# Second mixer of a two-layer trunk: output weights split in dead tiles during the attention, and another written order of squares and products in the last projection

## The chip, the cores and the metric

One core of one Trainium2 chip runs the whole program. The metric is device microseconds of one launch. The kernel before took 1179.97 us (median of three runs, 1178.41 to 1181.39).

## The reference

A decoder trunk of two layers on a sequence of 512 tokens, model width 1024, float32. Each layer is `x = x + rms_norm(mixer(rms_norm(x)))` and then `x = x + rms_norm(conv_ffn(rms_norm(x)))`. The change lies in the mixer of the second layer:

```python
def odd_mixer(h, w_in, w_out):
    cq, ck, cv, sq, sk, sv = split_cols(h @ w_in, ODD_SPLITS)
    o_dil = dilated_attention(groups(cq), groups(ck), groups(cv), slopes)   # 3 groups x 4 heads
    o_sb = stick_breaking_attention(heads_first(sq, 4), heads_first(sk, 4), heads_first(sv, 4))
    return concatenate([heads_last(o_dil), heads_last(o_sb)], axis=-1) @ w_out   # (512 x 512) @ (512 x 1024)
```

`dilated_attention` makes three softmax attentions per head over strided windows (group 0 with stride 1, groups 1 and 2 with strides 4 and 16) and merges them by weights made from their denominators: "the merged groups". The first 256 rows of `w_out` belong to the merged groups, the last 256 to stick-breaking.

## The kernel before

Every float32 product is made as three products of two-part numbers. A weight tile (128 x 1024) is loaded by SP into one of three buffers `wraw`; ACT casts it to the high part (`Weights.split`, L71), DVE subtracts to get the low part (L72); `mm3` (L253 to L255) issues three matmuls. The stream of weights `W` has five pairs of buffers `wh`/`wl` and splits five units ahead. A weight buffer is free again when its last matmul has run, a `wraw` buffer when DVE has subtracted.

Tokens are four tiles of 128, taken in `ORDER` 3, 2, 1, 0. `odd()` runs: projections and stick-breaking attention (pool `sb`: `sq`, `sk`, `sv`, the mask, the large tiles `z` and `sp`); then groups 1 and 2 (`score12`, `turn12`, `value12`, with table `tab12`), with the remaining projections as fillers between them; then sixteen small transfers `on<-ob` that put their results in token order; then group 0 (`score0`, `turn0`, `value0`, `merged`, one token tile each, in a pipeline of four stages by `skewed`), with the value projection `apv` as filler. `merged` transposes the merged output of a token tile and splits it into `og`.

Then follows the last projection. For each token tile, `row_product` makes twelve matmuls (`ao`, 128 x 512) for each of two halves of the output columns: six with the stick-breaking output `oS` and the two units of weights that come from `W`, six with `oG` and the two units that a second stream `W2` splits. `W2` is written behind the attention and has its own pool `owx`, whose memory overlaps that of `sb`. For each half, `part_of` then squares the product on ACT (L224, with a sum along the row) and multiplies it by a gain on DVE (L227). Then come the root (`rstd`, POOL, L177 to L180), the residual `X` (DVE, L1204), the mean square of the new `X` (ACT, L187), and the normalised tile `t` (`normed`, DVE, L1183). Eight PE transposes of `t` (L210), ACT casts (L170) and DVE subtractions (L171) put it into `xh`/`xl`, from which the second FFN starts with the products `u`.

Order: outside `manual_schedule` blocks a scheduler orders each engine's instructions when the program is built; inside (the last projection, for PE, DVE, ACT and POOL) the written order holds among the block's own instructions, and the scheduler mixes earlier ones in between. Each engine runs its instructions in that order.

Of the kernel before, what the change touches and what calls it, by code (L numbers as in the profile page):

```python
# [9 lines left out]
F32 = mybir.dt.float32  # L10
# [6 lines left out]
P = 128  # L17
S = 512
# [67 lines left out]
def trunk(tc, A, out):  # L86
# [3 lines left out]
    with ExitStack() as top:  # L90
# [125 lines left out]
        def part_of(t, ms, n, a, g, between=None):  # L216

            c = slice(n * S, n * S + S)
            o = t[:, c]
            if isinstance(a, tuple):  # L220
                DVE.tensor_tensor(o, *a, ALU.subtract)  # L221
                a = o
            junk = chp.tile([P, D], BF16, tag="junk", name="junk", bufs=1)
            ACT.activation(junk[:, :S], a, AF.Square, scale=D ** -0.5, accum_out=ms[:, n:n + 1])  # L224
            if between:
                between()
            DVE.tensor_tensor(o, a, g[:, c], ALU.mult)  # L227

        def begin(pool=None, tag="s"):
            return ((pool or chp).tile([P, D], F32, tag=tag, name="t"),  # L230
                    chp.tile([P, 2], F32, tag="ms", name="ms2", bufs=4))
# [630 lines left out]
        def odd(xnT, pending):  # L862
            xh, xl = xnT
            with ExitStack() as es:
# [13 lines left out]
                with ExitStack() as e1:  # L878
                    sb = e1.enter_context(tc.tile_pool(name="sb", bufs=1, reuse_waits="tile"))
                    sq = [sb.tile([P, S], F32, tag=f"sq{u}", name=f"sq{u}") for u in range(2)]  # L880
                    sk = [sb.tile([P, S], F32, tag=f"sk{u}", name=f"sk{u}") for u in range(2)]
                    sv = sb.tile([P, NT, 256], F32, tag="sv", name="sv")
                    smask = sb.tile([P, S], F32, tag="smask", name="smask")
                    tri = sb.tile([P, 2, P], F32R, tag="tri", name="tri")
                    trif = sb.tile([P, 2, P], F32, tag="z", name="trif", bufs=2)
                    nc.scalar.dma_start(smask[:], A["sb_mask"])
                    nc.scalar.dma_start(trif[:], A["sb_tri"])
                    DVE.tensor_copy(tri[:], trif[:])

                    def proj_T(dst, scale, permuted, on_act):  # L890
                        acc = bank("a", "apt")
                        wh, wl = W.next()
                        for k in range(KD):
                            mm3(acc[:], wh[:, k * P:(k + 1) * P], wl[:, k * P:(k + 1) * P],
                                xh[:, k], xl[:, k], k == 0, k == KD - 1)
                        src, d = acc[:], dst[:]
                        if permuted:
                            src = src.rearrange("p (t r) -> p r t", r=4)
                            d = d.rearrange("p (r t) -> p r t", r=4)
                        if on_act:  # L900
                            ACT.activation(d, src, AF.Copy, scale=scale)
                        else:
                            DVE.tensor_scalar(d, src, scale, None, ALU.mult)

                    def proj_V(dst):
                        ws = [W.next() for _ in range(2)]

                        def tile_V(i):
                            t = slice(i * P, (i + 1) * P)
                            a = bank("a", "apv")  # L910
                            for k in range(KD):
                                wh, wl = ws[k // 4]
                                c = slice((k % 4) * 256, (k % 4 + 1) * 256)
                                mm3(a[:, :256], xh[:, k, t], xl[:, k, t], wh[:, c], wl[:, c], k == 0, k == KD - 1)
                            if i % 2:
                                DVE.tensor_copy(dst[:, i], a[:, :256])
                            else:
                                ACT.copy(dst[:, i], a[:, :256])

                        return tile_V  # L920


                    ws = [W.next() for _ in range(4)]
                    for i in ORDER:
                        t = slice(i * P, (i + 1) * P)
                        a = bank("a", "av12")
                        for k in range(KD):
                            if k == KD // 2 and pending:
                                pending.pop(0)()
                            wh, wl = ws[k // 2]  # L930
                            c = slice((k % 2) * 512, (k % 2 + 1) * 512)
                            mm3(a[:], xh[:, k, t], xl[:, k, t], wh[:, c], wl[:, c], k == 0, k == KD - 1)
                        st = sb.tile([P, 512], F32, tag="sp", name="vst", bufs=2)
                        ACT.copy(st[:], a[:])
                        for r in range(4):
                            nc.scalar.dma_start(cv12[32 * i:32 * i + 32, r], st[r::4, :])


                    for u in range(2):
                        proj_T(sq[u], 0.125, False, True)  # L940
                        proj_T(sk[u], 1.0, False, False)
                    tile_V = proj_V(sv)
                    for i in ORDER:
                        tile_V(i)
                    off = (0, 512, 896, 1152, 1280)
                    spans = ((0, 0, 512), (1, 512, 896), (2, 896, 1280))

                    def sb_scores(u):

                        zs = [sb.tile([P, 1280], F32, tag="z", name="z", bufs=2) for _ in range(2)]  # L950
                        for n, (j0, o0, o1) in enumerate(spans):
                            zp = [bank(t, "zp") for t in ("ss", "nt", "ss")[n]]
                            for j in (j0,) if j0 < 2 else (2, 3):
                                for y in range(2):
                                    r = slice(y * 64, y * 64 + 64)
                                    PE.matmul(zp[y][:, off[j] - o0:off[j + 1] - o0], sk[u][r, j * P:(j + 1) * P],
                                              sq[u][r, j * P:], start=True, stop=True)
                            for y in range(2):
                                for j in (j0,) if j0 < 2 else (2, 3):
                                    DVE.tensor_tensor(zs[y][:, off[j]:off[j + 1]], zp[y][:, off[j] - o0:off[j + 1] - o0],  # L960
                                                      smask[:, :S - j * P], ALU.add)

                        sps = []
                        for z in zs:
                            sp = sb.tile([P, 1280], F32, tag="sp", name="sp", bufs=2)
                            DVE.tensor_scalar(sp[:], z[:], 40.0, None, ALU.min)
                            ACT.activation(sp[:], sp[:], AF.Exp)
                            sps.append(sp)
                        return list(zip(zs, sps))

                    def sb_softplus(z, sp):
                        ACT.activation(sp[:], sp[:], AF.Ln, bias=1.0)
                        DVE.tensor_tensor(sp[:], z[:], sp[:], ALU.max)

                    def sb_weights(z, sp):
                        sh = sb.tile([P, 1280], F32R, tag="sh", name="sh")
                        sl = sb.tile([P, 1280], F32R, tag="sl", name="sl")
                        split(sh[:], sl[:], sp[:])

                        for j0, o0, o1 in spans:  # L980
                            zp = bank("ssn"[j0], "cp")
                            for j in (j0,) if j0 < 2 else (2, 3):
                                n = S - j * P
                                c = off[j] - o0
                                for j2 in range(j, NT):
                                    for part in (sh, sl):
                                        PE.matmul(zp[:, c + (j2 - j) * P:c + n], tri[:, 0 if j2 == j else 1],
                                                  part[:, off[j2]:off[j2 + 1]], start=(j2 == j and part is sh),
                                                  stop=(j2 == NT - 1 and part is sl))
                            DVE.tensor_tensor(z[:, o0:o1], z[:, o0:o1], zp[:, :o1 - o0], ALU.add)  # L990
                        ACT.activation(z[:], z[:], AF.Exp)
# [325 lines left out]
```

## Time and profile before

| | |
|---|---|
| median of 3 runs | 1179.97 us (1178.41 to 1181.39) |
| profiled execution, own time | 1178.65 us |
| its span, first to last instruction | 1176.9 us |
| PE busy | 1152.7 us (98%) |
| PE weight loads busy | 942.3 us (80%) |
| DVE busy | 811.3 us (69%) |
| ACT busy | 557.0 us (47%) |
| HBM read and written | 117.95 and 6.29 MB, 106 GB/s |

The profile times one execution; "idle before, releaser" says what ended an engine's idle time. Times such as 790.83 are microseconds from the start of the span. The last projection starts at 786.2 and the second FFN at 820.2. The 1.75 us between own time and span lie outside the instructions.

### The profile page before, as it was taken

The page shows a single profiled execution, that of the slowest core. Times are in us where ns is not written, and L with a number is a line of the kernel's source. Part 1 is how long each engine was busy: PE and PEld are TensorE (multiplying, and loading weights), DVE is VectorE, ACT ScalarE, POOL GpSimd, SP SyncE. Part 2 cuts the span into 40 slices and gives each one's busy share as a digit, 9 for nine tenths or more (in the row PEclk, how much of TensorE's full clock was granted, in tenths as well). Part 3 has the DMA queues.
Part 4 walks back from the last instruction along what each step waited for, and adds up shares of the span by engine and source line. Part 5 has one row for each costly group of instructions (what it writes and reads, how often), then busy time and mean ns, then how long its engine had stood idle before and what let it go on. Part 6 is the DMA issues. An engine that isn't in the chain of part 4 may idle for free. (4 is left out here: it accounts for less than half of the span.)

```text
span 1176.9 us, 15162 instructions
## 1 busy us (share of the span) xinstructions
PE 1152.7 (98%) x5656; PEld 942.3 (80%) x5656; DVE 811.3 (69%) x1424; ACT 557.0 (47%) x942; POOL 56.7 (5%) x139
## 2 busy tenths in 40 slices
PE   8999999999999999999999999999999999999997
PEld 7876766798888888888878877887988888888885
DVE  6677358657666766899873465476576766779896
ACT  5465246445444434456553454454444434345562
POOL 2100002310000000000020000002000000000001
PEclk9999999999999999999999999999999999999999
DMA  7320340033233332354735212222233232324461
GB/s 284 109 81 19 114 126 1 37 129 122 94 92 105 90 103 86 100 158 159 245 110 154 72 54 93 69 55 108 94 109 106 90 107 90 95 94 135 142 207 72
DMA packets 39049, 126.81 MB, mean 108 GB/s; under 512 B 4672, under 2 KB 6336, under 8 KB 38848
## 3 DMA queue, kind: packets, MB, share of 16 engines
q1 hardware_dynamic: 37056, 122.11, 32.5%
q10 hardware_dynamic: 1920, 3.74, 1.0%
q8 instruction: 44, 0.72, 0.3%
q14 instruction: 29, 0.24, 0.1%
HBM read 117.95 MB, written 6.29 MB: 106 GB/s over the span
## 5 line engine op out<-in xcount | busy, mean ns | idle before, releaser
L72 DVE TENSOR_TENSOR wl<-wraw,wh 128x1024 fp32r<-128x1024 f32 (+1 forms) x205 | 248.2, 1218 | 186.5 <-ACT wh L71 185.9
L71 ACT CAST wh<-wraw 128x1024 fp32r<-128x1024 f32 (+1 forms) x205 | 212.6, 1046 | 289.5 <-PE u L254 177.8
L253 PE MATMUL u<-xh,wh 128*128 128x512 f32 (+1 forms) x768 | 285.0, 372 | 1.0 <-ACT xh L170 1.0
L254 PE MATMUL u<-xl,wh 128*128 128x512 f32 (+1 forms) x768 | 285.2, 372 | 0.7 <-DVE xl L171 0.7
L255 PE MATMUL u<-xh,wl 128*128 128x512 f32 (+1 forms) x768 | 285.0, 371 | 0.0
L253 PEld LDWEIGHTS u<-xh,wh 128*128 128x128 f32 x768 | 144.5, 188 | 26.3 <-ACT xh L170 1.4
L254 PEld LDWEIGHTS u<-xl,wh 128*128 128x128 f32 x768 | 144.7, 188 | 25.7 <-DVE xl L171 0.9
L255 PEld LDWEIGHTS u<-xh,wl 128*128 128x128 f32 x768 | 144.7, 188 | 25.0
L255 PE MATMUL acc<-wh,gl 128*128 128x512 f32 x248 | 96.5, 389 | 0.0
L254 PE MATMUL acc<-wl,gh 128*128 128x512 f32 x248 | 96.5, 389 | 0.0
L253 PE MATMUL acc<-wh,gh 128*128 128x512 f32 x248 | 96.4, 390 | 0.0
L402 ACT ACTIVATE y<-u,cw 128x512 f32<-128x512 f32 x88 | 67.6, 775 | 1.7 <-PE u L255 1.7
L407 ACT ACTIVATE y<-y 128x512 f32<-128x512 f32 x44 | 27.7, 632 | 85.1 <-DVE y L405 85.1
L405 DVE SCALAR_TENSOR_TENSOR y<-u,cw,y 128x510 f32<-128x510 f32 x88 | 65.6, 747 | 2.5
L403 DVE SCALAR_TENSOR_TENSOR y<-u,cw,y 128x511 f32<-128x511 f32 x88 | 65.1, 743 | 0.9 <-ACT y L402 0.9
L253 PEld LDWEIGHTS acc<-wh,gh 128*128 128x128 f32 x248 | 46.6, 188 | 10.1 <-issue 0.5
L255 PEld LDWEIGHTS acc<-wh,gl 128*128 128x128 f32 x248 | 46.6, 188 | 9.8
L254 PEld LDWEIGHTS acc<-wl,gh 128*128 128x128 f32 x248 | 46.6, 188 | 9.6
L253 PE MATMUL apt<-xh,wh 128*128 128x512 f32 x128 | 50.6, 396 | 0.0
L254 PE MATMUL apt<-xl,wh 128*128 128x512 f32 x128 | 50.0, 391 | 0.0
L255 PE MATMUL apt<-xh,wl 128*128 128x512 f32 x128 | 49.9, 390 | 0.0
L177 POOL TENSOR_TENSOR rv<-ms,epst 128x1 f32<-128x1 f32 x40 | 11.5, 291 | 734.8 <-ACT junk L224 668.8
(287 smaller groups left out, 1910.8 us busy)
## 6 DMA issues: line engine op xcount, KB each, us to landing
wraw<-in_ffn_w_up SPq DMA_DIRECT2D x88, 512.0 KB, 3.6
wraw<-in_ffn_w_down SPq DMA_DIRECT2D x44, 512.0 KB, 3.6
wraw<-in_od_w_dqk SPq DMA_DIRECT2D x12, 512.0 KB, 3.7
wraw<-in_ffn_w_down SPq DMA_DIRECT2D x22, 256.0 KB, 2.6
wraw<-in_ev_w_dqk SPq DMA_DIRECT2D x8, 512.0 KB, 3.7
wraw<-in_ev_w_out SPq DMA_DIRECT2D x8, 512.0 KB, 3.8
spill<-X SPq DMA_DIRECT2D x8, 512.0 KB, 2.6
X<-spill SPq DMA_DIRECT2D x8, 512.0 KB, 6.2
```

The lines of the kernel that those rows point to most:

```text
L71: self.nc.scalar.copy(h[:, :w], raw[:, :w])
L72: self.nc.vector.tensor_tensor(l[:, :w], raw[:, :w], h[:, :w].bitcast(F32), ALU.subtract)
L177: POOL.tensor_tensor(v[:, :n], ms, epst[:, :n], ALU.add)
L253: PE.matmul(o, lh, rh, start=first, stop=False, skip_group_check=more)
L254: PE.matmul(o, lh, rl, start=False, stop=False, skip_group_check=more)
L255: PE.matmul(o, ll, rh, start=False, stop=last, skip_group_check=more)
L402: ACT.activation(y[:, z], u, AF.Identity, bias=c[:, 3:4], scale=c[:, 2:3])
L403: DVE.scalar_tensor_tensor(y[:, z, 1:], u[:, :S - 1], c[:, 1:2], y[:, z, 1:], ALU.mult, ALU.add)
L405: DVE.scalar_tensor_tensor(y[:, z, 2:], u[:, :S - 2], c[:, 0:1], y[:, z, 2:], ALU.mult, ALU.add)
L407: ACT.activation(y[:, 0], y[:, 0], AF.Silu)
```

## The change

Four edits, all around the last projection of the second mixer:

1. The pool `sb` lives until the end of the mixer (its `with` block goes, and the code loses one step of indentation). `sq` and `sk` become one tile each instead of two.
2. `W2` is called before group 0 is written, and its high and low parts go into tiles that are read no more by then: unit 0 into `sq` and `sk`, unit 1 into `sv` and `tab12`. The pools `owx` and `osc` go, with one `spacer`.
3. The rows' tiles `t` come alternately from `z` and `sp` of pool `sb` (two buffers each) instead of three buffers of `osc`.
4. In a row of the last projection, the first half's product with the gain (DVE) is written ahead of its square (ACT), and the mean square of the row before is written after the first half's square instead of at the end of its own row. For the last row it stands behind the loop.

```diff
-        def part_of(t, ms, n, a, g, between=None):
+        def part_of(t, ms, n, a, g, between=None, dve_first=False):
...
+            def product():
+                DVE.tensor_tensor(o, a, g[:, c], ALU.mult)
+
+            if dve_first:
+                product()
             junk = chp.tile([P, D], BF16, tag="junk", name="junk", bufs=1)
             ACT.activation(junk[:, :S], a, AF.Square, scale=D ** -0.5, accum_out=ms[:, n:n + 1])
             if between:
                 between()
-            DVE.tensor_tensor(o, a, g[:, c], ALU.mult)
+            if not dve_first:
+                product()
...
-                with ExitStack() as e1:
-                    sb = e1.enter_context(tc.tile_pool(name="sb", bufs=1, reuse_waits="tile"))
-                    sq = [sb.tile([P, S], F32, tag=f"sq{u}", name=f"sq{u}") for u in range(2)]
-                    sk = [sb.tile([P, S], F32, tag=f"sk{u}", name=f"sk{u}") for u in range(2)]
+                sb = es.enter_context(tc.tile_pool(name="sb", bufs=1, reuse_waits="tile"))
+                sq, sk = [[t[:, u] for u in range(2)] for t in (sb.tile([P, 2, S], F32, tag="sq", name="sq"),
+                                                                sb.tile([P, 2, S], F32, tag="sk", name="sk"))]
...
+                W2 = Weights(nc, None, [(A["od_w_out"][k], 1024) for k in range(2)], 2, wpool)
+                homes = [[(sb, "sq"), (sb, "sk")], [(sb, "sv"), (ap, "tab12")]]
+                W2.pair = lambda: [pool.tile([P, D], F32R, tag=tag, name="wo") for pool, tag in homes.pop(0)]
+                wo2 = [W2.next() for _ in range(2)]
                 tile_V = proj_V(cv)
                 skewed([[g(i) for g in (score0, turn0, value0, merged)] for i in ORDER],
                        [lambda i=i: tile_V(i) for i in ORDER])
...
-                wx = es.enter_context(tc.tile_pool(name="owx", bufs=2, reuse_waits="tile"))
-                W2 = Weights(nc, wx, [(A["od_w_out"][k], 1024) for k in range(2)], 2, wpool)
-                wout = [W2.next() for _ in range(2)] + [W.next() for _ in range(2)]
-                sc = es.enter_context(tc.tile_pool(name="osc", bufs=3, reuse_waits="tile"))
-                spacer(sc, 16)
                 g_post, g_next = gain("od_post_g", 0), gain("ffn_pre_g", 1)
+                wout = wo2 + [W.next() for _ in range(2)]
...
-                        t, ms = begin(sc, "t")
+                        t, ms = begin(sb, ("z", "sp")[n % 2])
                         row_product(acc, terms, True, True, (0,))
-                        part_of(t, ms, 0, acc[0], g_post)
+                        part_of(t, ms, 0, acc[0], g_post, dve_first=True)
                         if n > 1:
                             turns.pop(0)()
+                        if n:
+                            j, tj = norms.pop()
+                            rj = mean_square(X[j][:])
                         row_product(acc, terms, True, True, (1,))
                         part_of(t, ms, 1, acc[1], g_post)
                         r = rstd(ms[:, 0:1], ms[:, 1:2])
                         if n:
-                            normed(*norms.pop())
+                            normed(j, rj, tj)
                         DVE.scalar_tensor_tensor(X[i][:], t[:], r[:, 0:1], X[i][:], ALU.mult, ALU.add)
-                        norms.append((i, mean_square(X[i][:]), t))
+                        norms.append((i, t))
                         turns.append(turned(i, nx, "na", t))
+
+                    r = mean_square(X[i][:])
```

In the built order, the first unit's cast and subtraction stand between the first and the second round of groups 1 and 2, the second unit's cast ahead of the last of the four exponentials of the second round, and its subtraction ahead of the last two copies `ob<-o`. On SP the order becomes: all four loads of `od_w_out`, four loads of `ffn_w_up`, then the sixteen `on<-ob`. Before, it was: two loads of `od_w_out`, two of `ffn_w_up`, two of `od_w_out`, then `on<-ob`, then the other two of `ffn_w_up`. PE's matmuls are the same in number; the `ao` products of the first row stand a little otherwise among the last transposes.

## The prediction

> **What bounds the kernel now.** I read the page first: which engine has no idle time.
>
> ```profile
> PE   8999999999999999999999999999999999999997
> PEclk9999999999999999999999999999999999999999
> ```
>
> PE is busy nearly everywhere, so this change can gain only where PE waits or runs slowly, and DVE or ACT time matters only where PE waits for it. The chain that ended last covers only the kernel's last 10 us, so PE's waits and its timeline come next. In the answer on all waits of PE (line, who ended it, us in total, times, longest), five rows touch the end of the second mixer (the first one's longer wait, 0.8, is the first mixer's).
>
> ```profile
> PE ao L253 <- ACT wh L71: 1.3, 2, 0.8
> PE ao L254 <- DVE wl L72: 1.1, 1, 1.1
> PE u L253 <- ACT xh L170: 1.0, 1, 1.0
> PE u L254 <- DVE xl L171: 0.7, 1, 0.7
> PE tpo L1162 <- ACT pt L1124: 0.5, 1, 0.5
> ```
>
> PE's timeline there (start, length, instruction, idle before it):
>
> ```profile
> 789.88 0.44 PE L1123 MATMUL t<-ident,s 128*128 128x128 f32 x2
> 790.83 0.44 PE L1162 MATMUL tpo<-ident,m 128*128 128x128 f32 x2 [0.52 <-ACT pt L1124]
> 792.57 0.51 PE L253 MATMUL ao<-wh,og 128*128 128x512 f32 x1 [0.46 <-ACT wh L71]
> 794.22 0.79 PE L254 MATMUL ao<-wl,og 128*128 128x512 f32 x1 [1.15 <-DVE wl L72]
> ...
> 800.20 0.39 PE L253 MATMUL ao<-wh,osh 128*128 128x512 f32 x1
> ...
> 818.77 0.39 PE L255 MATMUL ao<-wh,og 128*128 128x512 f32 x1
> 820.16 0.74 PE L253 MATMUL u<-xh,wh 128*128 128x256 f32 x4 [1.01 <-ACT xh L170]
> 821.56 0.38 PE L254 MATMUL u<-xl,wh 128*128 128x256 f32 x1 [0.66 <-DVE xl L171]
> ```
>
> The first row of the projection waits twice for the weights that `W2` splits last; later the FFN waits for the last normalised tile. The stretches of 5 us (PE busy, loads, DVE, ACT, POOL, granted clock, DMA) show a third loss.
>
> ```profile
> 785.00:790.00 5.00, 4.93 (x38) 4.28 (x38) 3.54 (x17) 2.69 (x9) 0.00 (x0) 1.00 0.27 97
> 790.00:795.00 5.00, 2.88 (x15) 2.09 (x16) 4.39 (x8) 2.70 (x5) 0.10 (x1) 0.91 0.38 107
> 795.00:800.00 5.00, 5.00 (x21) 3.94 (x20) 2.26 (x6) 1.75 (x6) 0.19 (x1) 0.75 0.61 210
> ```
>
> After the waits the clock is halved from about 794.0 to 797.4: products start 0.43 us apart instead of 0.227, which costs 3.4 x 0.5 = 1.7 us, in "busy" time. All these losses are a few tenths of a per cent of the span.
>
> **Part 1, the early split.** Four 128x1024 operations move (casts 1.05 us, subtractions 1.22 us). Where they go:
>
> - Cast and subtraction of unit 0 stand ahead of a cast of `W` and the second round's scores. SP issues its load at 734.13, where one of `ffn_w_up` was issued before; with the page's 3.5 us to landing it is there at 737.7, cast at 738.8, subtracted at 740.0. The scores started at 740.78 and now start about 1.1 us later, their exponentials too. PE takes the result only at 747.37, the last exponential began at 743.42: nothing on the path.
> - The cast of unit 1 waits for a load that SP can issue only when unit 0's subtraction has freed `wraw` (740.0): landed 743.5, cast 744.6. Queued behind it on ACT is the fourth exponential (0.51), now done near 745.3, and behind that only PE's transposes at 747.37. Cover 2 us; each microsecond beyond costs one.
> - Its subtraction falls into DVE's idle 3.40 us after 761.98, ahead of the copies `ob<-o` at 765.39. It frees the `wraw` for a fourth load of `ffn_w_up`, issued near 763.2 and landed near 766.7, ahead of the sixteen `on<-ob`, whose issue at 766.22 waits for those copies anyway. Perhaps 0.5 us late; DVE's `mn` waits for them (0.68 us before). Queued behind `mn` are the next scores, whose exponentials ended 1.8 us before PE's transposes at 777.03. So nothing.
> - At 783.2 one cast of `W` now precedes the last tile's exponentials (0.25 us later) and one subtraction the copy of `pt` (1.2 us later, to 786.4). PE needs that copy at 787.5, after the three `ao` products and two transposes that the built order now has there: nothing.
>
> What is left for PE from 786.02 to the second row: 24 products x 0.2275 = 5.46; 24 `o` matmuls 1.70 + 0.85; six pairs of transposes 1.3; seven returns from these to 512-wide products at 0.08 (0.31 against 0.23 to the next start), 0.6. Sum 9.9, with no late input: `og` is ready at 788.7 by the rows of cast and subtraction, its product comes at 790.0, and the wait for `pt` (0.52) is covered by three products that now lie in between. Before, it took 800.20 - 786.02 = 14.2. **Gain 4.2**, of which 1.7 is the clock.
>
> A rule speaks against counting that last part: in the Trainium skill, "TensorE: Matmul & The Clock Gate", section on HAM oscillation, only idle gaps over about 3.4 us throttle. By it these gaps (longest 1.15) would have cost no clock, and part 1 would gain 2.5. The trace disagrees, and I take the trace.
>
> **Part 2, the written order.** Per row, from one `X` to the next, a chain runs through DVE and ACT: product 0.69, square 0.69, casts `xh` 0.94, mean square 1.23, square to second product 0.73, product 0.60, `normed` 1.32, `X` 1.20: 7.4 us with `xh`, 6.5 without, against PE's 24 x 0.2275 = 5.46 (6.3 with transposes). Before, `X` followed `X` at 6.4, 7.05 and 8.35 us (802.14, 808.54, 815.59, 823.94). I laid the built order out with these lengths, PE's last product of the first row at 795.8:
>
> - Row 2: no wait; row 1: the transposes at 804.2 find `t` ready with 0.1 to spare.
> - Row 0: the transposes are due at 810.6, `t` has its halves at 811.4 and 812.1: PE waits 1.2 us in all, 0.6 more than before. **Loss 0.6**; its last product starts at 815.2.
> - FFN: a weight buffer comes free only with the third product of the last half (813.5), ACT casts into it (1.0), then squares (0.69), then casts `xh` (815.75): PE idle 0.4, then 0.3 for `xl`; it runs freely at 816.5. Before, from last product to free run were 2.8 us (818.77 to 821.56), now 1.35. **Gain 1.4**.
> - In the FFN's first 10 us the last two tiles' transposes are due about when `t` is (one was moved 20 products later in the built order). Waits of 0.1 + 0.1 + 0.2, taken as **loss 0.4**; later than that nothing.
>
> Tiles `t` in other memory: `X` at L242 and L1204, from two pools, takes 1283 and 1278 ns; I take 0, between -0.1 and +0.1 us.
>
> **Sum:** -4.2 + 0.6 - 1.4 + 0.4 = -4.6. The profiled execution, 1178.65 us (span 1176.9 and 1.75 around it), becomes 1174.0. It lies 1.3 below the median of the runs; off that median it is 1175.4, my forecast. Bounds: every wait gone, -4.2 and the 1.95 of `u` and `tp` before, about -6.2; clock unsaved, chain losses doubled and nothing gained at the FFN's start, -4.6 + 1.7 + 1.0 + 1.4 = -0.5.
>
> **Rivals.**
> - *The chain on DVE and ACT replaces PE as bound in the last projection.* For: its 7.4 against PE's 6.3, and `t` is found ready with 0.1 to spare. Against: laid out, it waits only in row 0. If the last two rows slip 1.2 each, 2.4 of the gain go: 1177.8, within 0.3%.
> - *The clock halves in another place.* Before, the 3.4 us ahead of 794.1 had 1.6 idle and half clock followed; those up to 821.4 had 1.5 idle and it did not, so the margin is thin. PE now idles 1.9 us in all between 810.6 and 816.6, spread over 6 us. One such stretch costs 1.7: 1177.1. The same title of the Trainium skill, section "What's actually happening", has the gate look at free-running windows of 3413 ns, by which some runs of before might escape the half clock and be 1.7 faster; the fastest run is only 0.24 below the profiled one, so none here shows that.
> - *Slower: the second unit's cast blocks ACT.* Place: ACT's queue at 743.5. Behind the cast stand an exponential and all of PE's next transposes. The Trainium skill, "PSUM — Partial Sum Buffer", section on engine and sequencer instructions, has ACT's queue strictly in order; ACT's rows here never overtake either. It costs one for one from 745.6 on, and 1.7 more of clock. To end 3.6 above the median before, it must cost 4.6 + 3.6 = 8.2, 6.5 beside the clock: landed at 752.1, 12 us after issue. Against: loads of this size landed in 3.5 to 4.4 us (medians of the page's groups). Then 1183.6.
> - *The early split is none*: if a tile that it needs is read later than I think, the 4.2 go and part 2 gains 0.4 alone: 1179.6. The built order puts the splits early; only a hidden wait could do it.
>
> **How the numbers follow.** Forecast 0.70; chain 0.12; clock 0.08; no early split 0.03; slower 0.07. A measurement of this kernel tells about 0.3%, 3.5 us, from no change: faster means below 1176.4. Of the forecast's 0.70 some 0.04 lies above that, as the runs before spread over 3 us (1178.4 to 1181.4); of the chain and clock cases 0.02 below. Faster 0.68, same 0.24, slower 0.08. The range: below, 1179.97 - 6.2 = 1173.8 less 1.0 for the spread, 1172.8; above, the chain's 1177.8 and 1.0, 1178.8.
>
> **What would show it.** Right: no wait of `ao` for `wh` or `wl`; PE's clock 1.00 from 780 to 820; the second row's first product near 796; `tp` waits for `t` in row 0; the first `u` near 815.9, free run at 816.5. Wrong: a PE wait for `pt` or `t` at 747 (cast on ACT), for `on` at 770 to 777, a stretch at half clock after 805, or `X` to `X` over 9 us in the first three rows.

## The result, and the profile after

| | before | after |
|---|---|---|
| median | 1179.99 us (12 runs, 1177.26 to 1181.39) | 1173.49 us (12 runs, 1172.20 to 1177.86) |
| profiled execution, own time | 1178.65 us | 1173.26 us |
| its span | 1176.9 us | 1171.4 us |

The ratio of the times is 0.9952, 95% interval 0.9941 to 0.9963: faster by 5.7 us of 1180, between 4.4 and 7.0 (the means lie 5.7 us apart, the medians 6.5). Beside other kernels on another occasion (e7 below) it was 0.9948 (0.9930 to 0.9967). Two slow executions are left out of all medians and ratios: one of e6, 1433 us at a mean clock of 0.75, and one of e7, 2956 us.

In the code after, `mm3` is L259 to L261, the square L229, the product with the gain L224, `normed` L1188, `X` L1212. PE's waits between 700 and 850 us (line, who ended it, us in total, times, longest):

```profile
PE tp L210 <- DVE t L1188: 0.7, 1, 0.7
PE u L259 <- ACT xh L170: 0.2, 1, 0.2
```

The five rows of before that the prediction lists are gone or shrunk: no `ao` waits for weights and no `tpo` for `pt`. The wait of the transposes `tp` for the normalised tile has grown from the 0.28 that it was before:

```profile
815.16 1.23 PE L210 MATMUL tp<-ident,t 128*128 128x128 f32 x8 [0.28 <-DVE t L1183]
```

PE's timeline of after shows where the time came from:

```profile
789.45 0.38 PE L1128 MATMUL t<-ident,s 128*128 128x128 f32 x2
789.59 0.48 PE L259 MATMUL ao<-wo,og 128*128 128x512 f32 x1
790.36 0.43 PE L1167 MATMUL tpo<-ident,m 128*128 128x128 f32 x2
...
795.56 0.39 PE L259 MATMUL ao<-wh,osh 128*128 128x512 f32 x1
...
811.11 1.23 PE L210 MATMUL tp<-ident,t 128*128 128x128 f32 x8 [0.69 <-DVE t L1188]
...
814.70 0.39 PE L261 MATMUL ao<-wo,og 128*128 128x512 f32 x1
815.24 0.74 PE L259 MATMUL u<-xh,wh 128*128 128x256 f32 x4 [0.15 <-ACT xh L170]
816.04 0.39 PE L260 MATMUL u<-xl,wh 128*128 128x256 f32 x1
```

The merged groups' weights (`wo`) are there when `og` is. The second row's first product starts at 795.56 instead of 800.20, and the FFN runs freely from 816.04 instead of 821.56. That difference, 5.5 us, is the whole difference of the spans. The stretches of 5 us (length, then PE busy, loads, DVE, ACT, POOL, granted clock, DMA):

```profile
785.00:790.00 5.00, 5.00 (x39) 4.57 (x39) 3.63 (x15) 1.71 (x8) 0.00 (x0) 1.00 0.61 199
790.00:795.00 5.00, 5.00 (x30) 3.88 (x29) 3.30 (x12) 1.93 (x7) 0.19 (x1) 1.00 0.01 2
795.00:800.00 5.00, 5.00 (x24) 4.17 (x24) 3.07 (x5) 1.60 (x5) 0.74 (x2) 1.00 0.08 32
```

PE is busy throughout where it had 2.88 of 5 us, and the clock column, 0.91 and 0.75 before, reads 1.00.

### The profile page after: what moved, and what is told of

The parts are those of the page before. It is cut to its first block, busy times and chain, and to the rows that moved or that the text cites. A ratio compares the mean times of both kernels' runs of the same rounds, so it can differ in the third digit from the quotient of the medians.

```text
span 1171.4 us, 15164 instructions
## 1 busy us (share of the span) xinstructions
PE 1151.1 (98%) x5656; PEld 941.4 (80%) x5656; DVE 811.3 (69%) x1424; ACT 556.9 (48%) x942; POOL 56.4 (5%) x138
## 5 line engine op out<-in xcount | busy, mean ns | idle before, releaser
L259 PE MATMUL u<-xh,wh 128*128 128x512 f32 (+1 forms) x768 | 285.1, 372 | 0.2 <-ACT xh L170 0.2
L261 PE MATMUL u<-xh,wl 128*128 128x512 f32 (+1 forms) x768 | 285.3, 372 | 0.0
L261 PEld LDWEIGHTS u<-xh,wl 128*128 128x128 f32 x768 | 144.7, 188 | 25.2
L259 PEld LDWEIGHTS u<-xh,wh 128*128 128x128 f32 x768 | 144.5, 188 | 25.4 <-ACT xh L170 0.6
L261 PE MATMUL acc<-wh,gl 128*128 128x512 f32 x248 | 96.6, 389 | 0.0
L259 PE MATMUL acc<-wh,gh 128*128 128x512 f32 x248 | 96.5, 390 | 0.0
L259 PEld LDWEIGHTS acc<-wh,gh 128*128 128x128 f32 x248 | 46.6, 188 | 10.1 <-issue 0.5
L261 PEld LDWEIGHTS acc<-wh,gl 128*128 128x128 f32 x248 | 46.6, 188 | 9.7
L259 PE MATMUL apt<-xh,wh 128*128 128x512 f32 x128 | 50.7, 396 | 0.0
L261 PE MATMUL apt<-xh,wl 128*128 128x512 f32 x128 | 49.9, 390 | 0.0
```

The source lines that it names most:

```text
L259: PE.matmul(o, lh, rh, start=first, stop=False, skip_group_check=more)
L261: PE.matmul(o, ll, rh, start=False, stop=last, skip_group_check=more)
```

## The experiments

All ratios are to the kernel before, run beside it on the same chip; 0.001 is 1.2 us. Before had a median of 1178.24 us beside e1 to e4 and of 1179.67 beside e5 to e8, so kernels of the two groups are compared by their ratios, not by their medians.

| | what | median us | ratio (95%) |
|---|---|---|---|
| e1 | early split, old written order | 1175.47 | 0.9969 (0.9959 to 0.9980) |
| e2 | new written order, late split | 1178.09 | 0.9995 (0.9986 to 1.0004) |
| e3 | after, square ahead of product | 1170.77 | 0.9938 (0.9923 to 0.9953) |
| e4 | after, mean square at its old place | 1173.28 | 0.9957 (0.9941 to 0.9973) |
| e5 | before, PE's wait filled | 1178.43 | 0.9988 (0.9975 to 1.0001) |
| e6 | e1, wait at the FFN's start filled | 1173.97 | 0.9945 (0.9925 to 0.9965) |
| e7 | after again | 1173.32 | 0.9948 (0.9930 to 0.9967) |
| e8 | e3 again | 1172.08 | 0.9932 (0.9911 to 0.9953) |

**e1: the early split alone.** The changed kernel with edit 4 undone:

```diff
-                        part_of(t, ms, 0, acc[0], g_post, dve_first=True)
+                        part_of(t, ms, 0, acc[0], g_post)
...
-                        if n:
-                            j, tj = norms.pop()
-                            rj = mean_square(X[j][:])
...
-                            normed(j, rj, tj)
+                            normed(*norms.pop())
...
-                        norms.append((i, t))
+                        norms.append((i, mean_square(X[i][:]), t))
```

> The early split with its homes in dead tiles and the tiles t in z and sp, but the last projection written as before (squares first, mean square at the end of its own row). Theory of the prediction: the two parts add up; the split brings 4.2 to 4.4 us (2.1 of waits of PE, 1.7 of half clock, the rest order among the last transposes), so 1175.6 against 1180.0. Rival, the chain on DVE and ACT binds as soon as the weights are early, and only the new written order lets the gain through: then the split alone brings under 3 us, 1177 or more. Rival, the split does nothing by itself: 1179.6.

Measured: 3.7 us faster (2.4 to 4.8). The weights' waits are gone as in the changed kernel, but the trace has a new loss. PE's timeline of e1:

```profile
814.33 0.74 PE L259 MATMUL u<-xh,wh 128*128 128x256 f32 x4 [1.04 <-ACT xh L170]
815.73 0.51 PE L260 MATMUL u<-xl,wh 128*128 128x256 f32 x1 [0.66 <-DVE xl L171]
816.04 0.42 PE L261 MATMUL u<-xh,wl 128*128 128x256 f32 x1
816.26 0.41 PE L260 MATMUL u<-xl,wh 128*128 128x256 f32 x1
```

The two waits at the FFN's start are those of before (1.01 and 0.66 there), but now products of 256 columns follow each other every 0.21 us instead of every 0.12: the clock is halved here, where before it was whole. The early split takes one stretch at half clock away and brings another. Up to there part 1 earns its whole price: counted from the start of the last scores `z` (782.71 before, 781.30 in e1), the second row (794.36) and the `u` at 815.73 both come 4.4 us earlier than before. The chain on DVE and ACT, the first rival, does not take that away; the clock behind it does.

**e2: the written order alone.** Before with edit 4 as in the diff of the change.

> The kernel before with only the new written order in the last projection (product ahead of square in the first half, mean square of the row before behind it); the weights of the merged groups are still split late, into their own pool. Theory of the prediction: 1.0 us (loss 0.6 at the row-0 transposes, gain 1.4 at the first FFN products), so 1179.0 against 1180.0, with the waits of ao for wh and wl and the stretch at half clock still there. Rival, the order is worth nothing without the split: 1180.0. Rival, the order carries most of the change: 1176 or less.

Measured: 0.6 us faster (1.7 faster to 0.5 slower), no change that can be told. The first `u` comes without a wait, but the `tp` transposes wait 0.66 for `t`, and in the profiled execution the stretch at half clock behind the weights' waits lasts 6.8 us instead of 3.4. In these stretches of 3.41 us the clock (third number from the right) is 0.50 twice:

```profile
789.73:793.14 3.41, 2.17 (x13) 1.48 (x13) 2.81 (x6) 2.39 (x5) 0.10 (x1) 1.00 0.30 52
793.14:796.56 3.42, 2.53 (x7) 2.04 (x8) 2.46 (x4) 0.79 (x3) 0.00 (x0) 0.50 0.68 242
796.56:799.97 3.41, 3.41 (x10) 2.63 (x10) 1.57 (x4) 1.06 (x5) 0.19 (x1) 0.50 0.45 169
```

**e5: is the half clock a price of PE's idle time?** Before, with five products that nobody reads in the wait of 1.15 us:

```diff
+                def filled(acc, terms):
+                    sp, (x, y, wh, wl) = bank("n", "spare"), terms[2]
+                    row_product(acc, terms[:2], True, False, (0,))
+                    PE.matmul(acc[0], x, wh[:, :S], start=False, stop=False)
+                    [PE.matmul(sp, terms[0][0], terms[0][2][:, :S], start=True, stop=True) for _ in range(5)]
+                    PE.matmul(acc[0], x, wl[:, :S], start=False, stop=False)
...
-                        row_product(acc, terms, True, True, (0,))
+                        row_product(acc, terms, True, True, (0,)) if n else filled(acc, terms)
```

> The kernel before, with five extra 128x512 products (read by nobody, into bank n) between the first row's product ao<-wh,og and ao<-wl,og, where PE waits 1.15 us for wl. Nothing else is changed. My theory (the half clock is a consequence of PE's idle time, and costs 1.7): the wait for wl is filled, wl is still ready at 794.2, the half-clock stretch near 794 to 797.5 is gone, and the time falls by 1.7 us, a ratio of 0.9986. Rival 1 (the half clock comes from something else than PE's idle time): the stretch stays, ratio 1.000. Rival 2 (the extra products cost: they delay the products behind them): ratio 1.000 to 1.001 with the clock whole.

PE's timeline and a stretch of 5 us of e5:

```profile
792.69 0.49 PE L1185 MATMUL ao<-wh,og 128*128 128x512 f32 x1 [0.46 <-ACT wh L71]
793.03 1.32 PE L1185 MATMUL spare<-wh,osh 128*128 128x512 f32 x5
794.35 0.50 PE L1185 MATMUL ao<-wl,og 128*128 128x512 f32 x1
```

```profile
795.00:800.00 5.00, 4.86 (x23) 3.65 (x22) 2.29 (x6) 2.19 (x8) 0.19 (x1) 1.00 0.65 210
```

The weights come no earlier (794.35 against 794.22), five products more are computed, and yet the second row starts at 799.24 instead of 800.20: the clock, 0.75 in this stretch before, is whole. The time, 1.4 us less (3.0 less to 0.1 more), agrees with the theory, though its interval just reaches no change; what settles it is the trace. The trace's own gain is smaller than the 1.7 expected: from `ao<-wl,og` to the second row it takes 4.89 us instead of 5.98, so 1.1. At whole clock PE comes early to the low part of the second unit of weights, which DVE finishes at 795.62; its product starts at 795.67, 0.53 behind the one ahead of it instead of 0.23.

**e6, with e9 and e10 for the traces: the same at the FFN's start.** e1 with four such products behind the last product of the last row.

```diff
+                def fill(n, q):
+                    spare = bank("o", "spare") if n == 3 else None
+                    [PE.matmul(spare, oS[0][:, 0, q], wout[2][0][:, :S], start=True, stop=True) for _ in range(4 * (n == 3))]
...
                         row_product(acc, terms, True, True, (1,))
+                        fill(n, q)
```

> The early split with the old written order (as e1_split_only), with four extra 128x512 products (read by nobody, into bank o) behind the last product ao of the last row, where PE waits 1.0 us for xh before the first u. In the trace of e1_split_only a stretch of 3.4 us at half clock follows this wait (815.8 to 819.3), which neither before nor after has there. My theory: what edit 4 adds to the early split in the changed kernel is mostly this stretch, so with the wait filled it goes and the ratio to before falls from 0.9969 to 0.9955, about the changed kernel's 0.9952. Rival (the written order itself shortens the way to the FFN, and the stretch is an accident of one execution): ratio 0.997, no change against e1_split_only.

Measured: 0.9945, where e1 had 0.9969 and 0.9955 was expected. The intervals touch, so the times alone do not settle it. e6 and e1 were run once more for their traces, as e9 and e10:

> e6_fill_ffn once more, for its trace. If the stretch at half clock after the FFN's start follows from PE's wait, the trace shows clock 1.00 from 800 to 830 and the extra products in the place of the wait for xh; if not, a stretch at half clock near 816 is there as in e1_split_only.

> e1_split_only once more, to see whether its stretch at half clock behind the wait for xh is regular. If it is, the trace shows 3.4 us at half clock that begin between 813 and 819; if it was an accident, clock 1.00 there.

The 5 us behind the FFN's start in e10 (early split alone, again):

```profile
815.00:820.00 5.00, 4.69 (x27) 4.69 (x28) 5.00 (x7) 0.92 (x2) 0.74 (x2) 0.66 0.36 122
```

and in e9 (its wait filled), with the extra products ahead of the first `u`:

```profile
815.00:820.00 5.00, 4.23 (x33) 4.03 (x34) 5.00 (x8) 2.42 (x6) 1.04 (x3) 1.00 0.33 105
```

```profile
813.90 1.07 PE L1190 MATMUL spare<-wh,osh 128*128 128x512 f32 x4
815.10 0.74 PE L259 MATMUL u<-xh,wh 128*128 128x256 f32 x4
816.51 0.39 PE L260 MATMUL u<-xl,wh 128*128 128x256 f32 x1 [0.67 <-DVE xl L171]
```

The stretch is in both traces of the early split alone (0.66 in e1 too) and is gone when the wait is filled. The two single times, 1175.48 (e9) and 1174.50 (e10), are in the opposite order, and the traces show why. e9 carries 3.4 us at half clock at the program's start that e10 does not have; its last scores start at 782.06 instead of 780.83. Counted from there, e9 is 1.5 us ahead behind the FFN's start, and it loses 1.3 of that again between 1118 and 1122, where its PE waits for `uu`, an operation of the FFN on DVE (L476), and that of e10 hardly does. So the clock that the filled wait saves is worth 1.5 us on the spot; how much of it the whole program keeps, one execution does not tell.

**e3, e4 and e8: which of edit 4's two moves does the work?** e4 puts the mean square back to the end of its own row and keeps `dve_first`; e3 keeps the mean square's new place and writes the square ahead of the product again:

```diff
-                        part_of(t, ms, 0, acc[0], g_post, dve_first=True)
+                        part_of(t, ms, 0, acc[0], g_post)
```

> The changed kernel with the mean square back at the end of its own row; the first half's product stays ahead of its square. Theory: ACT then waits for the last X ahead of the cast of xh, the first FFN products come 0.6 later although the row-0 transposes come 0.5 earlier: 1174.1 against 1173.5. Rival, the place of the mean square carries all of the order's gain: 1.0 to 1.4 slower than the changed kernel, 1174.5 to 1174.9. Rival, it is worth nothing: 1173.5.

> The changed kernel with the first half's square written ahead of its product again; the mean square stays in its new place. Laid out from the trace after: the square of row 1 starts at 803.9 instead of 806.1, the square of its second half 1.07 earlier, the row-0 transposes follow at 809.9 instead of 811.1, PE's wait of 0.69 there goes, and the FFN starts about 1.2 earlier: 1172.3 against 1173.5. Rival, the product first is what makes the new order good (the square would then stand on the path): slower than the changed kernel by the 1.4 credited to the FFN's start, 1174.9.

e4 came out 0.6 us slower than after by the ratios, far inside the intervals. Its trace has the wait of `u` for `xh` back (1.0) and the wait of `tp` down to 0.2: one loss for another, and the traces put the two kernels level (the table below). e3 came out 1.7 us faster than after by the ratios, and PE waits for nothing there between 700 and 850 us. As its profiled execution also lacks the half clock at the program's start, after and e3 were run again side by side:

> The changed kernel itself, unchanged, beside the next one on the same chip: ratio 0.995, 1173 to 1174 us.

> As e3_square_first: the changed kernel with the first half's square written ahead of its product again and the mean square kept in its new place. If it truly beats the changed kernel, it is 1.0 to 2.5 us faster than e7_after_again (about 1.0 by the waits of PE that it removes, the rest by clock); if the first comparison was luck with the clock at the program's start, the two are within 0.5 us.

e8 is 1.2 us faster than e7 by the medians, 1.9 by the ratios, whose intervals overlap; its profiled execution has the half clock at the start as that of after has, and its span is 1169.6 against 1171.4. The trace of e3 shows the same gain (the table below). So writing the product first is a loss. The reason is in ACT's and DVE's rows for the third row's first half. After:

```profile
804.15 1.27 DVE L1212 SCALAR_TENSOR_TENSOR X<-t,rr,X 128x1024 f32<-128x1024 f32 x1
805.34 0.68 DVE L224 TENSOR_TENSOR t<-ao,gain 128x512 f32<-128x512 f32 x1
806.14 0.60 ACT L229 ACTIVATE junk<-ao 128x512 bf16<-128x512 f32 x1 [3.98 <-DVE t L224]
806.73 1.07 ACT L170 CAST xh<-tp 128x512 fp32r<-128x512 f32 x2
```

and e8:

```profile
803.99 0.60 ACT L229 ACTIVATE junk<-ao 128x512 bf16<-128x512 f32 x1 [2.06 <-PE ao L261]
804.57 1.07 ACT L170 CAST xh<-tp 128x512 fp32r<-128x512 f32 x2
...
805.09 0.68 DVE L224 TENSOR_TENSOR t<-ao,gain 128x512 f32<-128x512 f32 x1
```

Both operations only read `ao`, but the one written second waits for the first; what makes a second reader wait, no run here shows. After, the first is DVE's, and DVE is busy with `X`; ACT idles 3.98 us and then squares, casts `xh` and takes the mean square 2.15 us later than it could. In e8 ACT squares as soon as PE is done, and DVE, which is late anyway, loses nothing.

**The traces side by side.** The time of a whole run also holds the stretch at half clock at the program's start, which comes and goes. This leaves it out: from the start of the last scores `z` to the start of PE's last product, in us, one execution each.

| before | e5 | e2 | e1, e10 | e9 | after, e7 | e4 | e3, e8 |
|---|---|---|---|---|---|---|---|
| 385.51 | 384.53 | 385.91 | 382.56, 383.20 | 383.00 | 380.37, 380.38 | 380.43 | 378.61, 378.55 |

Two traces of one kernel differ by 0.64, 0.01 and 0.06. By this table the early split alone is worth 2.3 to 3.0 us, both parts 5.1, and the square written first another 1.8. The mean square's place, with the product first, is worth nothing that shows (e4 against after).

## Why the prediction held, and where it didn't

- **The early split, gain 4.2.** The second row's first product comes 4.64 earlier, of which 0.26 was there before the last projection (the last scores `z` start at 782.45 instead of 782.71): 4.4.
- **1.7 of it clock.** The cause is right, by e5: filling one gap of 1.15 us gave the clock back. The size, 3.4 x 0.5, assumes that PE has its inputs during the whole stretch; e5's trace gives 1.1, as PE then comes early to a weight that is not ready, and e9 against e10, where the inputs are there, 1.5. The Trainium skill, "TensorE: Matmul & The Clock Gate", section on HAM oscillation, has as its rule no idle gaps of PE over about 3.4 us; here filling a gap of 1.15 us was enough, so the rows and not the rule decide.
- **The moved operations are covered.** Right. The second unit's cast began at 743.96 (forecast 743.5), the fourth exponential was done at 745.4 (forecast 745.3), and PE has no wait at 747. How much longer the cast could take before PE waits was not tried.
- **Row 0, PE waits 1.2 for `t`.** It waits 0.69; rows 2 and 1 do not wait, as laid out. From the second row's first product to the last product of the projection 0.57 us of the gain are lost, where 0.6 was forecast. With the mean square in its new place, the wait is the price of writing the product first (e8 has none), an order that the prediction had in its chain but did not question.
- **FFN.** Last product 814.70 (forecast 815.2), first `u` 815.24 (815.9), free run 816.04 (816.5). From last product to free run 1.34, forecast 1.35.
- **FFN's first 10 us, loss 0.4.** Did not occur: PE shows no wait there.
- **From sum to median.** Forecast 1175.4, measured 1173.5. Of the 1.9 between them 0.7 is the sum (1173.26 against 1174.0 for the profiled execution). The larger part is the shift to the median: the profiled execution lay 1.3 below the median before, and only 0.2 below it after.
- **The parts' shares.** Part 1 was priced at 4.2 and part 2 at 0.4. Alone they measure 3.7 and 0.6, together 5.7, and on top of part 1 part 2 is worth 2.0 by the ratios (0.9969 to 0.9952, intervals that just overlap) and 2.2 or 2.8 by the traces (e1 and e10 against after). The step that was missing: the forecast looked for a new half-clock stretch only in the finished kernel (rival 2), and there it is absent. In the kernel with part 1 alone it is there, and part 2 removes it along with the wait. Counted from the last scores, the `u` with `xl` comes 0.84 us earlier in after than in e1, which is the 1.4 less 0.6 of the forecast; most of the rest is the clock. So the sum came out for the whole kernel, and not for its parts.
- **The rivals.** The chain does not replace PE as the bound in the last two rows: `X` follows `X` by 6.65, 7.40 and 9.20 (797.50, 804.15, 811.55, 820.75), but the last interval holds the FFN's start, and PE waits 0.69 us for `t` in the last row, not the 1.2 in each of two rows that this rival needs. No ACT blocked, no half clock from 805 to PE's last product, and the early split is real.

## What to carry to other kernels

When two engines only read the same accumulator, look at which of them waits for the other: let the idle one read first and the busy one second; here that was worth 1.8 us. Count what PE idles in any stretch of about 3.4 us, not its longest gap: beside the wait itself, up to half of the next 3.4 us may be lost. And price each part of a change also without the other parts, since a wait that was harmless may turn costly when it moves.

## What was not expected of the hardware

In the eleven traces with a mean clock above 0.99 the granted clock changes only at multiples of 3.413 us from the trace's first change of it. In before the changes lie at 12.44, 15.86, 794.10, 797.52 and 1172.98 us: 0, 1, 229, 230 and 340 such steps. The Trainium skill, "TensorE: Matmul & The Clock Gate", section "What's actually happening", says that the gate looks at free-running windows of 3413 ns, and the traces agree. Whether a wait costs clock depends on how it falls into these windows. Four of them in the trace of before:

```profile
790.69:794.10 3.41, 1.78 (x11) 1.33 (x11) 2.80 (x6) 2.41 (x5) 0.00 (x0) 1.00 0.51 138
794.10:797.52 3.42, 3.30 (x9) 2.61 (x10) 1.99 (x5) 0.81 (x3) 0.00 (x0) 0.50 0.65 211
818.00:821.41 3.41, 1.89 (x10) 1.14 (x8) 2.33 (x3) 3.41 (x10) 1.47 (x4) 1.00 0.33 127
821.41:824.83 3.42, 3.27 (x28) 3.27 (x29) 3.42 (x6) 0.86 (x2) 0.66 (x2) 1.00 0.45 144
```

PE busy 1.78 of 3.41 is followed by half clock, 1.89 is not: the FFN's waits are cut by a window's border at 821.41. In e10, where the same waits fall into one window (PE busy 1.71), half clock follows. In e5 the filled window has 2.95 busy, and the clock stays whole. There is no sharp threshold: in e2 half clock follows 2.17 busy, and in e4 none follows 1.66 (7.15 to 10.56). What the gate sees beside PE's busy time stays open.

The clock also goes with most of the spread between runs: the after kernel's runs of 0.996 mean clock and more took 1172.2 to 1174.2 us, two runs of 0.995 took 1175.4 and 1176.1, and one of 0.992 took 1177.9; one stretch of 3.4 us at half clock is at most 1.7 us, or 0.0015 of the mean. Whether the program's start has such a stretch differs from one execution to the next: of one and the same kernel, e8's trace has it (12.66 to 16.08) and e3's does not.
